# Gates of a product-key expert layer: scattered into a DRAM table instead of built by one-hot matmuls

## The chip, the cores and the metric

The kernel runs on one core of a Trainium2 chip. The metric is the device time of one execution in microseconds. The five engines run side by side, each through its own queue of instructions in a fixed order: TensorE (PE; PEld are its weight loads), VectorE (DVE), ScalarE (ACT), GpSimd (POOL) and SyncE (SP, which here only issues DMAs). They wait for each other through semaphores.

## The reference, cut to what matters

Two transformer blocks over 272 and then 256 tokens of width 1024, all in float32. The change sits in the last part of the first block, a layer that routes each token to a few of 16384 experts:

```python
q = (xt @ w_q).reshape(BLOCK, PEER_HEADS, PEER_QDIM)            # 8 heads, 2 x 128 wide
s1 = einsum('chd,nd->chn', q[..., :half], keys1)                # 128 scores per head
s2 = einsum('chd,nd->chn', q[..., half:], keys2)                # 128 scores per head
t1, i1 = top_k(s1, 16);  t2, i2 = top_k(s2, 16)
cand = t1[..., :, None] + t2[..., None, :]                      # 256 sums
cidx = i1[..., :, None] * 128 + i2[..., None, :]                # expert number
ts, sel = top_k(cand, 16)
idx = take_along_axis(cidx, sel);  g = softmax(ts)
act = gelu(einsum('chkd,cd->chk', u[idx], xt))
return einsum('chk,chkd->cd', g * act, v[idx])
```

So a token has 8 heads of 16 experts each: 128 gates in all, of which two heads may name the same expert; then their gates add up.

## The kernel before, in words

**Dense form.** The kernel does not gather rows of `u` and `v`. It computes `u @ x` for all 16384 experts and 256 tokens (the first product), multiplies by a dense table of gates that is zero nearly everywhere, and multiplies the result with all of `v` (the second product). The table lives in the SBUF tile `C` of 128 x 128 x 256: partition `j` is the second key index, the middle index `a` the first key index, the last index the token. In the first product 64 steps `n` (two values of `a` each) fill it.

**Streams.** Every weight tile of 1 MB goes through `st.units` (line 115): SP loads it into one of two `raw` buffers (line 125), ACT copies a half of it in a rounded format into one of three `ws` buffers (line 138), DVE subtracts to get the rest (line 141), and PE runs three matmuls per pair (`mm3`, lines 157 to 159). One step `n` of the first product takes two such halves, 48 matmuls of 128x256.

**Routing** (lines 726 to 785). After each head's scores (line 848) DVE has two top-16 searches per head and token half (lines 732 to 737), the sums of the candidates (745), a third search (751 to 755), and a look-up of the expert numbers by comparison, product and sum over 16x50 elements (760 to 764). It runs for a whole token half `t` (128 tokens, 8 heads) at a time. PE then transposes key indices and gates (783), so that they lie in `idT` with one column per token.

**Scatter** (lines 787 to 806). For four tokens at a time DVE compares (789) to make one-hot rows of the second key index, ACT (795, 796) or DVE (798) makes one-hot rows of the first key index scaled by the gate, and PE multiplies the two (801): 128x128 gates of one token per matmul, 256 matmuls in all. DVE multiplies the part of `C` that is already there by it (804), ACT copies the rest into `C` (806), to be multiplied when the first product gets there (874).

**Order.** `work()` is a generator that yields after each piece with an estimated cost. After each step `n`, `advance` (line 831) takes pieces from it until their costs reach a limit that grows by `BUD` = 3.2 per step. `G` (line 723) ties a piece behind the last split of the weight stream. So the pieces of routing and scatter lie between the weight splits, in each engine's fixed queue.

Of the kernel before, what the change touches and what calls it, by code (L numbers as in the profile page):

```python
# [21 lines left out]
T = 256  # L22
# [11 lines left out]
NACT = 2  # L34
BUD = 3.2
RC = 1.3
R1STEP = 2
# [29 lines left out]
def _body(nc, tc, ctx, a, out, dbg):  # L67
# [30 lines left out]
    xd = dp.tile([128, 2, D], F32, name="xd")  # L98
    nc.sync.dma_start(X[0], a["x"][0:128])
# [4 lines left out]
    class Stream:  # L104
        def __init__(self):
            self.pools = [(gp, 2, 3)]
            self.gate = None
            self.reset()
# [6 lines left out]
        def units(self, src, alloc=None, eng=None, behind=None):  # L115
# [9 lines left out]
            nc.sync.dma_start(dst, src)  # L125
            res = []
# [140 lines left out]
    # ------------------------------------------------------------------ block 1  # L267
    with ExitStack() as s1:
# [14 lines left out]

        g1 = gain(G_NORM1, bp, bufs=1)
# [43 lines left out]
        # recurrent branch input and causal conv  # L328
# [15 lines left out]
        # latent projections  # L344
# [58 lines left out]
        # log_sigmoid(lambda) * 8  # L403
# [18 lines left out]
        # recurrent gates  # L422
# [41 lines left out]
        # keys, values, queries  # L464
# [90 lines left out]
        # recurrent output  # L555
# [7 lines left out]
        # attention, with other products between the heads  # L563
# [126 lines left out]
        finish(1)  # L690
        dump("h1", X[0])
        stop("h1")

    # ------------------------------------------------------------------ PEER
    with ExitStack() as s2:
# [8 lines left out]
        idT = cp.tile([128, 3, T], F32, name="idT")  # L704
        niota = cp.tile([128, 128], F32, name="niota")
        nc.vector.tensor_scalar(niota, iota, -1.0, None, ALU.mult)
        Tv = C[:, 112:120, 192:224].rearrange("p h (s k) -> p h s k", s=2)
        If = C[:, 120:128, 192:224].rearrange("p h (s k) -> p h s k", s=2)
        Iu = C[:, 120:128, 192:224].bitcast(U32).rearrange("p h (s k) -> p h s k", s=2)
        cand = C[:, 96:104, 128:128 + NCAND]  # L710
        cidx = C[:, 104:112, 128:128 + NCAND]
        eq = C[:, 112:128, 128:128 + NCAND]
        tsv = C[:, 112:120, 224:240]
        posu = C[:, 120:128, 224:240].bitcast(U32)
        posf = C[:, 120:128, 240:256]
        wks = [cp.tile([128, 128], F32, name=f"wk{i}") for i in range(2)]
        sl = cp.tile([128, 3, 8, 16], F32, name="sl")
        sli = cp.tile([128, 2, 128], I32, name="sli")

        def bc(v, k):  # L720
            return v.unsqueeze(3).to_broadcast([128, v.shape[1], v.shape[2], k])
# [4 lines left out]
        def routing(t):  # L726
            V = nc.vector
            for s in range(16):
                h, k = s // 2, s % 2
                src = sc[t][:, s, :]  # L730
                wk1 = wks[s % 2]
                G(V.max(Tv[:, h, k, 0:8], src))
                V.max_index(Iu[:, h, k, 0:8], Tv[:, h, k, 0:8], src)
                V.match_replace(wk1, Tv[:, h, k, 0:8], src, -3.4e38)
                yield 0.5
                G(V.max(Tv[:, h, k, 8:16], wk1))
                V.max_index(Iu[:, h, k, 8:16], Tv[:, h, k, 8:16], wk1)
                yield 0.35
            V.tensor_copy(If, Iu)
            V.tensor_scalar(If[:, :, 0, :], If[:, :, 0, :], 128.0, None, ALU.mult)  # L740
            yield 0.6
            for src, dst in ((Tv, cand), (If, cidx)):
                for i0, ni, nj, o in CAND:
                    d = dst[:, :, o:o + ni * nj].rearrange("p h (i j) -> p h i j", i=ni)
                    V.tensor_tensor(out=d, in0=bc(src[:, :, 0, i0:i0 + ni], nj),
                                    in1=src[:, :, 1, 0:nj].unsqueeze(2).to_broadcast([128, 8, ni, nj]), op=ALU.add)
                yield 1.6
            for h in range(8):
                c = cand[:, h, :]
                wk1 = wks[h % 2]  # L750
                G(V.max(tsv[:, h, 0:8], c))
                V.max_index(posu[:, h, 0:8], tsv[:, h, 0:8], c)
                V.match_replace(wk1[:, :NCAND], tsv[:, h, 0:8], c, -3.4e38)
                V.max(tsv[:, h, 8:16], wk1[:, :NCAND])
                V.max_index(posu[:, h, 8:16], tsv[:, h, 8:16], wk1[:, :NCAND])
                yield 0.8
            V.tensor_copy(posf, posu)
            fidx = sl[:, 0]
            for h in range(8):
                G(V.tensor_tensor(out=eq, in0=posf[:, h, :].unsqueeze(2).to_broadcast([128, 16, NCAND]),  # L760
                                  in1=iota[:, :NCAND].unsqueeze(1).to_broadcast([128, 16, NCAND]), op=ALU.is_equal))
                yield 0.9
                G(V.tensor_tensor(out=eq, in0=eq, in1=cidx[:, h, :].unsqueeze(1).to_broadcast([128, 16, NCAND]), op=ALU.mult))
                V.tensor_reduce(fidx[:, h, :], eq, AX.X, ALU.add)
                yield 1.8
            f2 = fidx.rearrange("p h k -> p (h k)")
            V.tensor_copy(sli[:, 0], f2)
            V.tensor_scalar(sli[:, 1], sli[:, 0], 127, None, ALU.bitwise_and)
            V.tensor_scalar(sli[:, 0], sli[:, 0], 7, None, ALU.logical_shift_right)
            V.tensor_scalar(sl[:, 0].rearrange("p h k -> p (h k)"), sli[:, 0], -1.0, None, ALU.mult)  # L770
            V.tensor_copy(sl[:, 1].rearrange("p h k -> p (h k)"), sli[:, 1])
            yield 0.8
            e = sl[:, 2]
            V.tensor_tensor(out=e, in0=tsv, in1=tsv[:, :, 0:1].to_broadcast([128, 8, 16]), op=ALU.subtract)
            nc.scalar.activation(e, e, AF.Exp)
            sm = small.tile([128, 8], F32, name="sm", tag="sm", bufs=2)
            V.tensor_reduce(sm, e, AX.X, ALU.add)
            V.reciprocal(sm, sm)
            V.tensor_tensor(out=e, in0=e, in1=sm.unsqueeze(2).to_broadcast([128, 8, 16]), op=ALU.mult)
            yield 0.6  # L780
            p = ps("pt")
            for j in range(3):
                nc.tensor.transpose(p[:, j * 128:(j + 1) * 128], sl[:, j].rearrange("p h k -> p (h k)"), ident)
            nc.scalar.activation(idT[:, :, t * 128:(t + 1) * 128], p[:, :384].rearrange("p (j t) -> p j t", j=3), AF.Copy)
            yield 0.1

        def scatter(t0, bound):
            oh = x_tile().rearrange("p (q w) -> p q w", q=4)
            G(nc.vector.tensor_tensor(out=oh[:, :, 0:128], in0=iota.unsqueeze(1).to_broadcast([128, 4, 128]),
                                      in1=idT[:, 1, t0:t0 + 4].unsqueeze(2).to_broadcast([128, 4, 128]), op=ALU.is_equal))  # L790
            for k in range(4):
                t = t0 + k
                o = oh[:, k, 128:256]
                if k < NACT:
                    nc.scalar.activation(o, iota, AF.Abs, bias=idT[:, 0, t:t + 1])
                    nc.scalar.activation(o, o, AF.Relu, bias=idT[:, 2, t:t + 1], scale=-4.0)
                else:
                    G(nc.vector.tensor_scalar(o, niota, idT[:, 0, t:t + 1], idT[:, 2, t:t + 1], ALU.is_equal, ALU.mult))
            p = ps("pm")
            for k in range(4):  # L800
                nc.tensor.matmul(p[:, k * 128:(k + 1) * 128], oh[:, k, 0:128], oh[:, k, 128:256], start=True, stop=True)  # L801
            v = p.rearrange("p (q a) -> p a q", q=4)
            cs = C[:, 0:bound, t0:t0 + 4]
            nc.vector.tensor_tensor(out=cs, in0=v[:, 0:bound, :], in1=cs, op=ALU.mult)
            if bound < 128:
                nc.scalar.activation(C[:, bound:128, t0:t0 + 4], v[:, bound:128, :], AF.Copy)

        r0, r1 = routing(0), routing(1)

        class Scattered:  # L810
            done = 0

        def work():
            for c in r0:
                yield c * RC
            for k in range(64):
                if k == 32:
                    for c in r1:
                        yield c * RC
                scatter(4 * k, work.bound)  # L820
                Scattered.done = 4 * k + 4
                yield 1.1 + work.bound / 240
                for _ in range(R1STEP if k < 32 else 0):
                    c = next(r1, None)
                    if c:
                        yield c * RC

# [3 lines left out]
        def advance(limit):  # L831
            while spent[0] < limit:
                c = next(todo, None)
                if c is None:
                    return
# [652 lines left out]
```

## Time and profile before

| what | value |
|---|---|
| three timed runs | 2146.55, 2145.16, 2147.39 us; median 2146.55 |
| span of the profiled execution | 2144.5 us; the runs lie 0.7 to 2.9 us above it |
| mean granted TensorE clock | 0.995 |
| busy share of POOL | 5% |
| HBM traffic | 360.29 MB read, 2.10 MB written, 169 GB/s over the span |

A busy share is an average over the whole span. The first block takes the first 290 us, the projection `wpq` and the scores end near 346 us, the first product runs to 771 us, the second product to about 1123 us, and the second block takes the rest. What a change is worth is read from the stage it touches.

### The profile page before, as it was taken

Reading aid. Unit: us, or ns where it says so; the run is one execution under the profiler, and the core shown is the slowest. Engines: PE = TensorE matmul, PEld = TensorE weight load, DVE = VectorE, ACT = ScalarE, POOL = GpSimd, SP = SyncE. Lnnn points to the kernel's source line nnn. Section 1 sums busy time; section 2 is a strip of 40 time slices with the busy share of each in tenths; the row PEclk is TensorE's granted clock in tenths of the full one; section 3 lists DMA queues with packets and bytes.
Section 4 is the critical chain, followed back from the end, with each engine's and each line's share of the span. In section 5 each row is a group of like instructions: output and inputs, shape, how many; then the busy total and the mean of one; then the engine's idle time right before and its main releaser. Section 6 shows DMA issues by size and latency. Waiting matters only on the chain.

```text
span 2144.5 us, 31162 instructions
## 1 busy us (share of the span) xinstructions
PE 2093.2 (98%) x12401; PEld 1838.8 (86%) x12401; DVE 1395.0 (65%) x2361; ACT 1143.7 (53%) x1903; POOL 113.6 (5%) x112
## 2 busy tenths in 40 slices
PE   8989999999999999999999999999999999999998
PEld 7889989999999988888887887887887888887886
DVE  6685668888888865555557555967556554756554
ACT  5875444576657744444446444665445444555443
POOL 2010000000000000000000000840000000000000
PEclk9999999999999999999999999999999999999999
DMA  6432554544443445555576554316554654634551
GB/s 212 160 124 96 175 175 163 185 154 159 171 162 137 147 167 191 183 195 184 189 261 230 190 184 170 118 40 248 193 180 170 217 179 157 225 120 165 188 183 72
DMA packets 65361, 365.57 MB, mean 170 GB/s; under 512 B 6704, under 2 KB 8880, under 8 KB 33472
## 3 DMA queue, kind: packets, MB, share of 16 engines
q1 hardware_dynamic: 65216, 363.59, 49.1%
q8 instruction: 97, 1.59, 0.3%
q14 instruction: 48, 0.39, 0.1%
HBM read 360.29 MB, written 2.10 MB: 169 GB/s over the span
## 4 chain that ended last, share of the span: by engine, by line
PE 87%; DVE 5%; ACT 4%; DMA 2%; issue 1%; POOL 1%; SPq 0%; POOLq 0%; DVEq 0%; ACTq 0%
PE pa L157 18%; PE pa L159 18%; PE pa L158 18%; PE pm L157 8%; PE pm L159 8%; PE pm L158 8%; PE pm L801 3%; DVE ws L141 2%; PE pt L194 2%; PE pm L1106 1%; ACT ws L138 1%; DMA raw<-in_ffn_dram 1%; POOL rr L180 1%; ACT sq L170 1%; PE pm L590 1%
## 5 line engine op out<-in xcount | busy, mean ns | idle before, releaser
L141 DVE TENSOR_TENSOR ws<-raw,ws 128x1024 fp32r<-128x1024 f32 (+1 forms) x653 | 795.7, 1225 | 519.8 <-ACT ws L138 514.9
L138 ACT ACTIVATE ws<-raw 128x1024 fp32r<-128x1024 f32 (+1 forms) x657 | 689.3, 1057 | 548.2 <-PE pa L159 347.2
L157 PE MATMUL pa<-xT,ws 128*128 128x256 f32 x1280 | 365.0, 286 | 0.0
L159 PE MATMUL pa<-xT,ws 128*128 128x256 f32 x1280 | 360.9, 282 | 0.0
L158 PE MATMUL pa<-xT,ws 128*128 128x256 f32 x1280 | 360.8, 282 | 0.0
L157 PE MATMUL pm<-ws,xT 128*128 128x512 f32 (+1 forms) x768 | 298.9, 389 | 2.3 <-ACT xT L162 2.3
L159 PE MATMUL pm<-ws,xT 128*128 128x512 f32 (+1 forms) x768 | 294.7, 384 | 2.3 <-DVE xT L163 2.2
L158 PE MATMUL pm<-ws,xT 128*128 128x512 f32 (+1 forms) x768 | 293.8, 383 | 1.1 <-DVE ws L141 1.0
L157 PEld LDWEIGHTS pa<-xT,ws 128*128 128x128 f32 x1280 | 242.1, 189 | 0.3 <-ACT xT L162 0.3
L158 PEld LDWEIGHTS pa<-xT,ws 128*128 128x128 f32 x1280 | 242.0, 189 | 0.0
L159 PEld LDWEIGHTS pa<-xT,ws 128*128 128x128 f32 x1280 | 241.9, 189 | 0.0
L157 PE MATMUL pa<-ws,ch 128*128 128x512 f32 x512 | 201.3, 395 | 1.0 <-ACT ch L162 1.0
L158 PE MATMUL pa<-ws,ch 128*128 128x512 f32 x512 | 201.9, 395 | 0.0
L159 PE MATMUL pa<-ws,ch 128*128 128x512 f32 x512 | 201.5, 394 | 0.0
L159 PEld LDWEIGHTS pm<-ws,xT 128*128 128x128 f32 x768 | 144.8, 189 | 33.0 <-DVE xT L163 3.5
L157 PEld LDWEIGHTS pm<-ws,xT 128*128 128x128 f32 x768 | 144.9, 189 | 30.3 <-ACT xT L162 4.0
L158 PEld LDWEIGHTS pm<-ws,xT 128*128 128x128 f32 x768 | 144.8, 189 | 29.9 <-DVE ws L141 2.5
L157 PE MATMUL pa<-ws,hT 128*128 128x512 f32 x352 | 141.9, 403 | 0.6 <-ACT hT L162 0.5
L159 PE MATMUL pa<-ws,hT 128*128 128x512 f32 x352 | 137.9, 394 | 0.2
L158 PE MATMUL pa<-ws,hT 128*128 128x512 f32 x352 | 137.7, 391 | 0.0
L180 POOL TENSOR_TENSOR rr<-rs,mhalf 128x1 f32<-128x1 f32 (+1 forms) x36 | 28.7, 798 | 1938.9 <-DVE rs L178 1938.9
L157 PEld LDWEIGHTS pa<-ws,ch 128*128 128x128 f32 x512 | 96.4, 188 | 23.6 <-ACT ch L162 1.2
(390 smaller groups left out, 3202.1 us busy)
## 6 DMA issues: line engine op xcount, KB each, us to landing
raw<-in_ffn_dram SPq DMA_DIRECT2D x132, 1024.0 KB, 4.9
raw<-in_peer_u_dram SPq DMA_DIRECT2D x64, 1024.0 KB, 4.9
raw<-in_peer_v_dram SPq DMA_DIRECT2D x64, 1024.0 KB, 4.9
raw<-in_win_dram SPq DMA_DIRECT2D x16, 1024.0 KB, 4.8
gain<-in_gains_dram SPq DMA_DIRECT2D x17, 512.0 KB, 5.6
raw<-in_wpq_dram SPq DMA_DIRECT2D x8, 1024.0 KB, 5.0
raw<-in_wcin_dram SPq DMA_DIRECT2D x8, 1024.0 KB, 4.9
raw<-in_wrnn_dram SPq DMA_DIRECT2D x4, 1024.0 KB, 4.9
```

The lines of the kernel that those rows point to most:

```text
L138: i = nc.scalar.activation(hi, r, AF.Copy)
L141: self.last = (eng or nc.vector).tensor_tensor(out=lo, in0=r, in1=hi.bitcast(F32), op=ALU.subtract)
L157: nc.tensor.matmul(o, wh, xh, start=first, stop=False)
L158: nc.tensor.matmul(o, wh, xl, start=False, stop=False)
L159: nc.tensor.matmul(o, wl, xh, start=False, stop=last)
L170: nc.scalar.activation(sq[:rows, :p.shape[-1]], p, AF.Square, accum_out=ss[:rows, i:i + 1])
L180: nc.gpsimd.tensor_tensor(out=r2[:rows], in0=r[:rows], in1=mhalf[:rows], op=ALU.pow)
L194: nc.tensor.transpose(p[:, j * rows:(j + 1) * rows], src[:rows, (b + j) * 128:(b + j + 1) * 128], ident[:rows, :rows])
L590: nc.tensor.matmul(sp[:, :nk], qT[h // 8][:, h % 8, t * 128:(t + 1) * 128], kT[h // 8][:, h % 8, :nk], start=True, stop=True)
L801: nc.tensor.matmul(p[:, k * 128:(k + 1) * 128], oh[:, k, 0:128], oh[:, k, 128:256], start=True, stop=True)
L1106: in_turn(nc.tensor.matmul(p[:, :T], dg, u[:, k:k + T], start=k == 0, stop=k == 30))
```

## The change

- A DRAM tile `gd` of 128 x (128 x 256) takes the place of the one-hot products. Sixteen DMAs of 1 MB each set it to zero during the first block. They come from the SP queue, one after each call of the weight stream from the 8th on.
- Routing is done for one head and one token half at a time, heads in the outer loop, as soon as the scores of a head are there. Its scratch tiles lie outside `C`.
- The expert number is computed as an address in `gd` that includes the token. The 16 gates of a head and token half are added into `gd` by 16 indirect DMAs of 128 elements each, issued by POOL: 256 in all. Those of one group are declared independent, those of the next head of the same tokens wait for the ones before. In POOL's queue each indirect DMA also waits for the completion of the one eight places ahead of it.
- The transposes, the one-hot rows, the one-hot matmuls and both ways of multiplying in the first product go. `C` holds the activated first product alone.
- In the second product POOL reads 512 KB of `gd` for four values of `a` at a time (32 reads), and DVE multiplies that part of `C` by it, one group ahead of its use.
- The softmax uses one ACT instruction per head and token half, with the sum accumulated there.
- `BUD` goes from 3.2 to 3.0 without the factor 1.3 on routing; before the first product a limit of 1.5 per head holds.

Core of the diff (line numbers of the new kernel differ by a few to some tens from those of the old one):

```diff
+    gd = dp.tile([128, 128 * T], F32, name="gd")
...
+            self.calls += 1
+            if self.aside is not None:
+                self.aside(self.calls)
...
+        zero = tmp("zero", [128, 512], 1)
+        nc.gpsimd.memset(zero, 0.0)
+        def clear(i):
+            i -= ZFROM
+            if 0 <= i < ZN:
+                w = 128 * T // ZN
+                nc.sync.dma_start(gd[:, i * w:(i + 1) * w].rearrange("p (r w) -> p r w", w=512),
+                                  zero.unsqueeze(1).to_broadcast([128, w // 512, 512]))
...
+            V.tensor_scalar(If[:, z, 0, :], Iu[:, z, 0, :], float(T), tokf[:, t:t + 1], ALU.mult, ALU.add)
+            V.tensor_scalar(If[:, z, 1, :], Iu[:, z, 1, :], 128.0 * T, None, ALU.mult)
+            for src, dst in ((Tv, cand), (If, cidx)):
+                for i0, ni, nj, o in CAND:
+                    d = dst[:, z, o:o + ni * nj].rearrange("p (i j) -> p i j", i=ni)
+                    V.tensor_tensor(out=d, ...)
...
+            nc.scalar.activation(e, tsv[:, z, :], AF.Exp, bias=nm, accum_out=sm)
...
+            for k in range(16):
+                i = nc.gpsimd.indirect_dma_start(gflat, bass.IndirectOffsetOnAxis(ap=slot[:, t, h, k:k + 1], axis=0),
+                                                 gate[:, t, h, k:k + 1], None, compute_op=ALU.add)
...
-        def scatter(t0, bound):
-            oh = x_tile().rearrange("p (q w) -> p q w", q=4)
-            G(nc.vector.tensor_tensor(out=oh[:, :, 0:128], ..., op=ALU.is_equal))
-            for k in range(4):
...
-            for k in range(4):
-                nc.tensor.matmul(p[:, k * 128:(k + 1) * 128], oh[:, k, 0:128], oh[:, k, 128:256], start=True, stop=True)
...
+        def work():
+            for h in range(8):
+                yield h, 0.0
+                for t in range(2):
+                    for c in routing(t, h):
+                        yield h, c
...
-            advance(13.6 + BUD * (n + 1) if n < 62 else 1e9)
+            nc.scalar.activation(C[:, 2 * n:2 * n + 2, :], p.rearrange("p (a t) -> p a t", a=2), AF.Gelu_apprx_tanh)
+            advance(WQBUD * 7 + BUD * (n + 1) if n < 36 else 1e9)
...
+        def gates_of(g):
+            v = x_tile().rearrange("p (a t) -> p a t", a=4)
+            nc.gpsimd.dma_start(v, gd[:, 4 * T * g:4 * T * (g + 1)].rearrange("p (a t) -> p a t", a=4))
+            return v
+        def gated_c(g):
+            c = C[:, 4 * g:4 * g + 4, :]
+            nc.vector.tensor_tensor(out=c, in0=c, in1=gl.pop(0), op=ALU.mult)
+            if g + 2 < 32:
+                gl.append(gates_of(g + 2))
```

How the change moves instructions is read from the order of each engine's queue. The first place is DVE in the middle of the first product. `ws<-raw,ws` are the splits of the weight stream, the others belong to the scatter; before, with the kernel's old line numbers:

```order
L141 TENSOR_TENSOR ws<-raw,ws 128x1024 x2
L874 TENSOR_TENSOR C<-hb,C 128x2x196
L804 TENSOR_TENSOR C<-pm,C 128x112x4
L789 TENSOR_TENSOR x<-iota,idT 128x4x128
L804 TENSOR_TENSOR C<-pm,C 128x112x4
L798 TENSOR_SCALAR x<-niota,idT 128x128 x2
```

And now, near step 23 of the first product, the later part of one head's routing (`tsv` the 16 best sums, `eqs` the look-up, `gate` the gates), with the new line numbers:

```order
L148 TENSOR_TENSOR ws<-raw,ws 128x1024
L771 MAX tsv<-cand 128x8
L772 MAX_INDEX posu<-tsv,cand 128x8
L773 MATCH_REPLACE wk_3145<-tsv,cand 128x50
L777 TENSOR_SCALAR nm<-tsv 128x1
L774 MAX tsv<-wk_3145 128x8
L780 MAX_INDEX posu<-tsv,wk_3145 128x8
L781 CAST posf<-posu 128x16
L783 TENSOR_TENSOR eqs<-posf,iota 128x800
L786 TENSOR_TENSOR eqs<-eqs,cidx 128x800
L790 RECIPROCAL sm<-sm 128x1
L148 TENSOR_TENSOR ws<-raw,ws 128x1024 x2
```

Routing now fills the room between the splits in steps 0 to 34 in place of the scatter's pieces, and none is left after the split of step 34. The first address (`slot`) is finished on DVE between the splits of the sixth and the seventh of the eight `wpq` tiles.

The second place is POOL's queue around this layer. Before, ten of the small powers of the norms (line 180) follow each other there, two ahead of this layer and eight behind it; then comes the convolution of the second block (1147):

```order
L363 TENSOR_TENSOR qr_979<-ropet 128x16x16
L180 TENSOR_TENSOR rr<-rs,mhalf 128x1 x10
L1147 TENSOR_TENSOR pw<-ud,pv 128x1024
L1150 TENSOR_TENSOR pw<-pw 128x512 x2
L1147 TENSOR_TENSOR pw<-ud,pv 128x1024
```

Now:

```order
L381 TENSOR_TENSOR qr_986<-ropet 128x16x16
L187 TENSOR_TENSOR rr<-rs,mhalf 128x1 x2
L740 IOTA tok 128x2
L794 DMA gd<-gate,slot 4194304x1 x256
L864 DMA x<-gd 128x1024 x32
L187 TENSOR_TENSOR rr<-rs,mhalf 128x1 x8
L1132 TENSOR_TENSOR pw<-ud,pv 128x1024
```

The 256 indirect DMAs and the 32 reads stand between the second and the third of these powers, all in one queue, the reads behind the last indirect DMA.

The third place is SP's queue early in the first block, where weight tiles (`raw`) are loaded. Before:

```order
L125 DMA raw<-in_win_dram 128x2048 x2
L565 DMA mask<-in_mask_dram 128x416
L90 DMA iota<-in_iota_dram 128x128
L186 DMA gain<-in_gains_dram 128x1024
L125 DMA raw<-in_win_dram 128x2048 x2
L125 DMA raw<-in_wkn_dram 128x2048
```

Now:

```order
L129 DMA raw<-in_win_dram 128x2048 x2
L298 DMA gd<-zero 128x4x512
L129 DMA raw<-in_win_dram 128x2048
L298 DMA gd<-zero 128x4x512 x3
L129 DMA raw<-in_win_dram 128x2048
L298 DMA gd<-zero 128x4x512
L129 DMA raw<-in_wkn_dram 128x2048
```

Five of the sixteen clearing DMAs come here, three of them in a row ahead of one weight tile; three small loads have moved behind.

## Rows read from the trace of the kernel before

**Rows 1.** The page, part 1: busy us (share of the span) and instructions of each engine.
```profile
PE 2093.2 (98%) x12401; PEld 1838.8 (86%) x12401; DVE 1395.0 (65%) x2361; ACT 1143.7 (53%) x1903; POOL 113.6 (5%) x112
```
**Rows 2.** The chain that ended last, first line by engine, second by line.
```profile
PE 87%; DVE 5%; ACT 4%; DMA 2%; issue 1%; POOL 1%; SPq 0%; POOLq 0%; DVEq 0%; ACTq 0%
PE pa L157 18%; PE pa L159 18%; PE pa L158 18%; PE pm L157 8%; PE pm L159 8%; PE pm L158 8%; PE pm L801 3%; DVE ws L141 2%; PE pt L194 2%; PE pm L1106 1%; ACT ws L138 1%; DMA raw<-in_ffn_dram 1%; POOL rr L180 1%; ACT sq L170 1%; PE pm L590 1%
```
**Rows 3.** Busy us by stretch; the columns are in the first line.
```profile
core 0: us, PE busy (x) PEld busy (x) DVE busy (x) ACT busy (x) POOL busy (x), PEclk, DMA share, GB/s
305.00:352.00 47.00, 47.00 (x403) 47.00 (x402) 38.26 (x139) 20.33 (x30) 0.00 (x0) 1.00 0.47 158
352.00:433.00 81.00, 81.00 (x686) 81.00 (x684) 70.71 (x170) 40.40 (x49) 0.00 (x0) 1.00 0.55 184
439.00:770.00 331.00, 330.62 (x2815) 330.21 (x2813) 275.62 (x622) 218.91 (x505) 0.00 (x0) 1.00 0.45 153
771.50:1107.00 335.50, 335.50 (x1445) 272.05 (x1444) 182.30 (x153) 156.70 (x152) 0.00 (x0) 1.00 0.55 188
```
**Rows 4.** ACT in order of time, ends of steps: start us, us, engine, line [idle before].
```profile
351.63 0.60 ACT L876 ACTIVATE C<-pa 128x512 f32<-128x512 f32 x1 [0.49 <-PE pa L159]
358.22 0.60 ACT L876 ACTIVATE C<-pa 128x512 f32<-128x512 f32 x1 [1.73 <-PE pa L159]
426.57 0.60 ACT L876 ACTIVATE C<-pa 128x512 f32<-128x512 f32 x1 [1.78 <-PE pa L159]
432.27 0.60 ACT L876 ACTIVATE C<-pa 128x512 f32<-128x512 f32 x1 [1.79 <-PE pa L159]
770.55 0.58 ACT L873 ACTIVATE hb<-pa 128x512 f32<-128x512 f32 x1
```
**Rows 5.** The chain of waits late in the first product: start us, us, what.
```profile
755.60 1.78 PE pm L801 x16
763.08 0.89 PE pm L801 x8
```
**Rows 6.** DVE groups by form: count, busy us, mean ns, idle before them.
```profile
L141 DVE TENSOR_TENSOR ws<-raw,ws 128x1024 fp32r<-128x1024 f32 x46 | 56.0, 1220 | 24.2 <-ACT ws L138 24.2
L840 DVE COPY C<-pa 128x256 f32<-128x256 f32 x16 | 6.0, 414 | 0.2
```
**Rows 7.** DVE in order of time near 350 us.
```profile
349.77 1.22 DVE L141 TENSOR_TENSOR ws<-raw,ws 128x1024 fp32r<-128x1024 f32 x1
350.91 0.29 DVE L736 MAX8 C<-wk 128x8 f32<-128x128 f32 x1
356.08 0.53 DVE L745 TENSOR_TENSOR C<-C 128x32 f32<-128x32 f32 x4
```
**Rows 8.** POOL in order of time, then DVE beside the last two.
```profile
1123.33 0.55 POOL L180 TENSOR_TENSOR rr<-rs,mhalf 128x1 f32<-128x1 f32 x1 [833.29 <-DVE rs L178]
1132.38 1.46 POOL L180 TENSOR_TENSOR rr<-rs,mhalf 128x1 f32<-128x1 f32 x1 [5.12 <-DVE rs L178]
1453.88 2.60 POOL L180 TENSOR_TENSOR rr<-rs,mhalf 128x1 f32<-128x1 f32 x1 [10.80 <-DVE rs L178]
1132.21 1.22 DVE L141 TENSOR_TENSOR ws<-raw,ws 128x1024 fp32r<-128x1024 f32 x1
1454.85 1.22 DVE L141 TENSOR_TENSOR ws<-raw,ws 128x1024 fp32r<-128x1024 f32 x1
```
**Rows 9.** DMA issues: count, KB each, median us from issue to landing.
```profile
raw<-in_win_dram SPq DMA_DIRECT2D x16, 1024.0 KB, 4.8
gain<-in_gains_dram SPq DMA_DIRECT2D x17, 512.0 KB, 5.6
```
**Rows 10.** Table loads of ACT in the first product.
```profile
L876 ACT ACT_TABLE_LOAD  x2: 1283/1283/1283, 349.9 to 379.4; - x2
```
**Rows 11.** Waits of PE up to 295 us: total us, times, longest.
```profile
PE pa L159 <- DVE ws L141: 5.6, 3, 2.7
```

More of the change, by code (lines that the diff above doesn't have):

```diff
@@ L33 @@
 NCAND = 50
[L34 to L37, printed above, removed]
+BUD = 3.0
+WQBUD = 1.5
+ZFROM = 8
+ZN = 16
 NTAP = (16, 16, 16, 16)
@@ L107, in __init__ @@
             self.gate = None
+            self.calls = 0
+            self.aside = None
             self.reset()
@@ L690, in _body @@
         finish(1)
+        st.aside = None
+        assert st.calls >= ZFROM + ZN
         dump("h1", X[0])
@@ L711, in _body @@
[L711 to L721, printed above, removed]
+        NC = 2
@@ new lines, in _body @@
+        wks = [cp.tile([128, 128], F32, name=f"wk{i}") for i in range(NC)]
+        Tv = cp.tile([128, NC, 2, 16], F32, name="Tv")
+        Iu = cp.tile([128, NC, 2, 16], U32, name="Iu")
+        If = cp.tile([128, NC, 2, 16], F32, name="If")
+        cand = cp.tile([128, NC, NCAND], F32, name="cand")
+        cidx = cp.tile([128, NC, NCAND], F32, name="cidx")
+        tsv = cp.tile([128, NC, 16], F32, name="tsv")
+        posu = cp.tile([128, NC, 16], U32, name="posu")
+        posf = cp.tile([128, NC, 16], F32, name="posf")
@@ new lines, in _body @@
+        fid = cp.tile([128, NC, 16], F32, name="fid")
+        eqs = cp.tile([128, 16, NCAND], F32, name="eqs")
+        gate = cp.tile([128, 2, 8, 16], F32, name="gate")
+        slot = cp.tile([128, 2, 8, 16], I32, name="slot")
+        tok = cp.tile([128, 2], I32, name="tok")
+        tokf = cp.tile([128, 2], F32, name="tokf")
+        nc.gpsimd.iota(tok, [[128, 2]], base=0, channel_multiplier=1)
+        nc.vector.tensor_copy(tokf, tok)
+        gflat = gd.rearrange("p (e o) -> (p e) o", o=1)
@@ L723, in G, with routing @@
         def G(i):
             after(i, st.last)
-        def routing(t):
+        def routing(t, h):
             V = nc.vector
[L728 to L741, printed above, removed]
+            z = t
+            for k in range(2):
+                src = sc[t][:, 2 * h + k, :]
+                wk1 = wks[z]
+                G(V.max(Tv[:, z, k, 0:8], src))
+                V.max_index(Iu[:, z, k, 0:8], Tv[:, z, k, 0:8], src)
+                V.match_replace(wk1, Tv[:, z, k, 0:8], src, -3.4e38)
+                yield 0.6
+                G(V.max(Tv[:, z, k, 8:16], wk1))
+                V.max_index(Iu[:, z, k, 8:16], Tv[:, z, k, 8:16], wk1)
+                yield 0.4
+            V.tensor_scalar(If[:, z, 0, :], Iu[:, z, 0, :], float(T), tokf[:, t:t + 1], ALU.mult, ALU.add)
+            V.tensor_scalar(If[:, z, 1, :], Iu[:, z, 1, :], 128.0 * T, None, ALU.mult)
@@ L757, in routing @@
[L757 to L765, printed above, removed]
@@ L775, in routing @@
[L775 to L783, printed above, removed]
@@ L808, in _body @@
[L808 to L826, printed above, removed]
+                    d = dst[:, z, o:o + ni * nj].rearrange("p (i j) -> p i j", i=ni)
@@ new lines, in routing @@
+            nm = small.tile([128, 1], F32, name="nm", tag="nm", bufs=2)
+            sm = small.tile([128, 1], F32, name="sm", tag="sm", bufs=2)
+            V.tensor_scalar(nm, tsv[:, z, 0:1], -1.0, None, ALU.mult)
+            e = gate[:, t, h, :]
+            nc.scalar.activation(e, tsv[:, z, :], AF.Exp, bias=nm, accum_out=sm)
+            V.max_index(posu[:, z, 8:16], tsv[:, z, 8:16], wk1[:, :NCAND])
+            V.tensor_copy(posf[:, z, :], posu[:, z, :])
+            yield 0.9
+            G(V.tensor_tensor(out=eqs, in0=posf[:, z, :].unsqueeze(2).to_broadcast([128, 16, NCAND]),
+                              in1=iota[:, :NCAND].unsqueeze(1).to_broadcast([128, 16, NCAND]), op=ALU.is_equal))
@@ new lines, in routing @@
+            yield 0.9
+            G(V.tensor_tensor(out=eqs, in0=eqs, in1=cidx[:, z, :].unsqueeze(1).to_broadcast([128, 16, NCAND]), op=ALU.mult))
+            yield 0.9
+            G(V.tensor_reduce(fid[:, z, :], eqs, AX.X, ALU.add))
+            V.tensor_copy(slot[:, t, h, :], fid[:, z, :])
+            V.reciprocal(sm, sm)
+            V.tensor_scalar(e, e, sm, None, ALU.mult)
+            yield 1.2
+            for k in range(16):
+                i = nc.gpsimd.indirect_dma_start(gflat, bass.IndirectOffsetOnAxis(ap=slot[:, t, h, k:k + 1], axis=0), gate[:, t, h, k:k + 1], None,
+                                                 compute_op=ALU.add)
+                for key in [(t, h)] + [(1 - t, g) for g in range(h + 1)]:
+                    tc.declare_no_dep(i.ins, group="gates%d.%d" % key, reason="other elements")
+                tc.add_to_no_dep_group("gates%d.%d" % (t, h), i.ins)
@@ L828, in _body, with advance @@
+        def work():
+            for h in range(8):
+                yield h, 0.0
+                for t in range(2):
+                    for c in routing(t, h):
+                        yield h, c
         todo = work()
         spent = [0.0]
[L831 to L835, printed above, removed]
-                spent[0] += c
+        nxt = [next(todo)]
+        def advance(limit, heads=8):
+            while nxt[0] is not None and nxt[0][0] < heads and spent[0] < limit:
+                spent[0] += nxt[0][1]
+                nxt[0] = next(todo, None)
@@ L867, in _body @@
                 scores(7)
[L868 to L880 removed]
+            nc.scalar.activation(C[:, 2 * n:2 * n + 2, :], p.rearrange("p (a t) -> p a t", a=2), AF.Gelu_apprx_tanh)
+            advance(WQBUD * 7 + BUD * (n + 1) if n < 36 else 1e9)
+        assert nxt[0] is None
         acc = [[ps("pa") for _ in range(2)] for _ in range(2)]
```

73 lines of the change are left out of this document (15 added, 58 removed).

## The prediction

> **What bounds the kernel now.** I read four views in this order: the page's busy times, the chain of waits, the busy time by stretch, and the pace of the steps. The page has PE at 2093.2 us of a span of 2144.5 [rows 1], and the chain that ended last is PE for 87% [rows 2]. That is an average, so the stage of the change counts. In the stretch from 439 to 770 us, where the scatter runs, PE is busy 330.62 of 331.00 us, DVE 275.62, POOL not at all, at full clock [rows 3]. The same holds before the scatter starts (352 to 433 us: PE 81.00 of 81.00, DVE 70.71) and in the second product (335.50 of 335.50). So each matmul that goes in this stage gives its time back, as long as nothing else becomes late.
>
> **What the change removes.** The pace without scatter is read from the ends of the steps: step 1 at 358.22, step 14 at 432.27 us, which is 74.05 us for 13 steps, 5.70 us each [rows 4]. Step 0 ended at 351.63, and the last one, step 63, at 770.55. At the bare pace the 63 steps between would take 358.9 us; the last scores (8 matmul records, 6.59 us for step 1 instead of 5.70) add 0.9. The stage took 418.9. The rest, 59.2 us, is what scatter and transposes cost PE. A second way agrees: the chain has 8 records of the one-hot product as a piece of 0.89 us and 16 as 1.78 [rows 5]; 64 such pieces are 57.0 us, and the six transposes and small waits make up the other two. I take 59.2 us off.
>
> **What it adds on DVE.** The pieces of routing stay, and the scatter's DVE work goes, but routing now has to fit into the room beside the splits within 35 steps. The room: two splits start 1.14 us apart from what follows them (349.77 and 350.91 [rows 7]), so a step leaves 5.70 - 2.28 = 3.42 us. The need: from 305 to 433 us DVE was busy 38.26 + 70.71 = 109.0 us [rows 3]; 45 splits (128 us at half a step of 2.85) at 1.22 us make 54.9, and the 16 copies of the projection 6.0 [rows 6]. What is left, 48 us, is the routing of one token half, 96 for both. By head, the 14 sums of candidates are issued 16 x 14 times instead of 2 x 14: 196 more at 0.13 us (four in 0.53 us [rows 7]) are 26 us. Seven small instructions per head and half in place of some eleven per half are about 90 more, 12 us. Together 134 us, an estimate, of which a tenth (58 of 624 instructions in the order) falls into the projection before. So 121 us in 35 steps, 3.46 us against 3.42 of room: DVE is full and about 1.4 us short, and bunches add something. From below the cost is nothing, since `ws` buffers give some lead; from above, with instructions that wait for the one before them a quarter dearer (1.22 us for a split that costs 1.14 in a stream, 0.29 for a search that costs 0.20), routing is 168 us, 151 of it in the stage, and 151 + 35 x 2.28 = 231 against 199 us of steps: 32 us late. I take 3 us, near the measured pace of routing.
>
> **ACT.** The sixteen exponentials now stand between activations of the other kind. One table load is 1.28 us [rows 10]; some 28 of them are 36 us in 35 steps, 1.0 us a step. With two copies of 1.06 and one activation of 0.60 [rows 4] a step needs 3.8 of 5.70 us. Nothing, while ACT has this room; if an exponential has to wait for DVE at a bad moment, the copy behind it and then PE wait, which is part of the 32 us above.
>
> **The clearing DMAs.** Sixteen of 1 MB stand in SP's queue among the weight loads of the first block. One such transfer lands in 4.8 us [rows 9], and at one place three stand ahead of a weight tile. In all of the first 295 us PE waited for splits in its main products 5.6 us, in three waits [rows 11], so loads have some lead, though not everywhere. Bounds: nothing, and 3 x 4.8 = 14.4 us. I take 2.
>
> **The second product.** DVE gets 32 products of the size of a split, 39 us over the stage of some 350; it is busy 182.30 of 335.50 us there, so it goes to about 65%. POOL's 32 reads of 512 KB add a quarter to the 2 MB of weights per group, and the DMA engines are at 0.55 [rows 3]. Both are one group (about 21 us) ahead of their use and cost nothing; without that lead each group would pay 1.2 us, 39 in all.
>
> **The indirect DMAs: the open price.** None is in the trace. The first address is ready when DVE is through the seventh `wpq` tile at the latest, near 330 us by the place in the order, and the first product would now end at 770.6 - 59.2 + 3 + 2 = 716 us. The first read of the table needs all 256 of them and then lands in about 5.6 us (512 KB [rows 9]). So they are hidden if one takes POOL up to (716 - 330 - 5.6) / 256 = 1.49 us. The last address comes with step 34, near 548 us, so the pace of routing does not bind. The nearest rows are POOL's smallest instruction, over 128x1: 0.55 us with DVE idle beside it, 1.46 beside one split, 2.60 beside two instructions of DVE, ending 0.41 us after DVE's in both cases [rows 8]. DVE is busy five sixths of this stretch while routing runs, and less than half of it afterwards. The bounds are 0.55 and 2.60; I take 1.46, the row with one split beside it, which matches two splits per step. Then POOL is through at 330 + 374 = 704 us and the table is there at 710, 6 us before it is needed. The cover is thin: each 0.1 us more per DMA is 26 us later.
>
> The rows show POOL held until DVE's instruction ends. [...]
>
> **Sum.** Against the profiled execution's span of 2144.5: - 59.2 + 3 + 2 = 2090.3 us. The median of the runs lies 2.05 us above that span, so 2092 us.
>
> **Rivals.**
> - *POOL is late, and the kernel is slower.* Mechanism: each indirect DMA waits for DVE, the first read of `gd` stands behind all of them in POOL's queue, DVE's first product with the gates waits for the read, and PE's second product for DVE. For it: 1.46 and 2.60 us in rows 8, and DVE at 85% there. Against it: from step 35 on DVE runs only two splits a step, 2.4 of 5.7 us, and 163 us of the stage are left. At the middle of the two rows, 2.03 us, the table is there at 330 + 520 + 5.6 = 856 us, 140 late: 2232 us. At 2.60 it is 1001, 2377 us. It decides from 1.70 us on: then the 54 us of net gain are gone.
>
> [...]
>
> - *DVE is the bound of the first product.* For it: 85 to 87% busy before, and need equal to room above. Against it: PE did not wait with DVE at 87%. Price: the 32 us bound instead of 3, 2121 us.
> - *The matmuls were hidden anyway,* and the time stays at 2146: then PE would have had idle time in the stage, but it has 0.4 of 331 us. PE would have to wait elsewhere for what it no longer does.
>
> **How the numbers follow.** The forecast (2080 to 2115) has 0.58. DVE as the bound 0.11. POOL late 0.28: of that 0.05 between 1.49 and 1.70 us and still faster, 0.02 about equal, 0.21 slower. Hidden anyway 0.03, 0.01 of it equal and 0.02 slower. Within 0.2% (4.3 us) is about what a measurement of this kernel cannot tell from no change. So faster 0.74, same 0.03, slower 0.23. The range: down to 2080, where nothing that is added costs and the scheduling of the first block gains some us; up to 2180, which takes in DVE's bound and POOL up to 1.83 us per DMA. The likeliest case alone is 2080 to 2115.
>
> **What would show it.** Right: no matmul between the three of the weight stream, steps of 5.7 us from 1 to 63, the first product ending near 716 us, POOL's last indirect DMA before that, and PE going on into the second product with no more than a us or two of waiting. Steps of 6 us or more up to step 34 with DVE ahead of PE in the waits: DVE was mis-sized. A gap of PE between the products, released through the read of `gd`: the price of the indirect DMAs was wrong, and its size divided by 256 says by how much. PE waits on splits before 250 us that were not there: the clearing DMAs.

## The result, and the profile after

The changed kernel takes 2385.31 us (median of 4 runs, 2384.30 to 2388.88) against 2145.86 us before: a ratio of 1.1115, interval 1.1102 to 1.1128. The forecast of 2092 us and its range up to 2180 us missed it; the rival "POOL is late" had the way from POOL to PE, but at its middle price a wait of 140 us, half of what came. The matmuls did go. The page of the changed kernel, part 1, answers to [rows 1]:

```profile
PE 2040.5 (86%) x11883; PEld 1784.1 (75%) x11883; DVE 1345.4 (56%) x2372; ACT 1088.2 (46%) x1588; POOL 562.7 (24%) x402
```

PE has 52.7 us less to do, and is busy for 86% of the span instead of 98%. The busy time by stretch shows where it stands idle (columns as in [rows 3]: PE, PEld, DVE, ACT, POOL, then PE's granted clock, DMA share, GB/s):

```profile
352.00:433.00 81.00, 81.00 (x683) 80.81 (x682) 79.82 (x314) 54.16 (x69) 69.96 (x37) 1.00 0.67 179
439.00:567.00 128.00, 127.80 (x1074) 127.33 (x1073) 114.97 (x421) 81.61 (x99) 110.01 (x60) 1.00 0.71 188
567.00:847.00 280.00, 0.50 (x5) 0.29 (x3) 3.22 (x3) 1.54 (x2) 228.42 (x151) 0.51 0.25 4
847.00:1006.00 159.00, 152.59 (x1246) 150.71 (x1246) 97.95 (x83) 67.84 (x77) 15.12 (x29) 0.98 0.78 271
```

Up to 567 us PE is as full as before, although DVE is busy 79.82 of 81 us instead of 70.71. Then everything but POOL stops for 280 us. It stops in the middle of the first product, and not behind it. ACT in order of time, ends of steps 0, 1, 37, 38 and 63, answers to [rows 4]:

```profile
354.49 0.60 ACT L847 ACTIVATE C<-pa 128x512 f32<-128x512 f32 x1 [0.42 <-issue]
361.07 0.60 ACT L847 ACTIVATE C<-pa 128x512 f32<-128x512 f32 x1 [1.78 <-PE pa L166]
...
567.29 0.60 ACT L847 ACTIVATE C<-pa 128x512 f32<-128x512 f32 x1 [1.78 <-PE pa L166]
855.19 0.60 ACT L847 ACTIVATE C<-pa 128x512 f32<-128x512 f32 x1 [1.81 <-PE pa L166]
...
1006.17 0.58 ACT L847 ACTIVATE C<-pa 128x512 f32<-128x512 f32 x1
```

Who holds PE is read backwards through two engines. PE waits for a split of DVE (waits of PE from 346 to 1010 us: total us, times, longest):

```profile
PE pa L166 <- DVE ws L148: 285.4, 10, 279.9
```

DVE in order of time (three splits, then the stop) shows that the next split stood behind a product of `C` with the gates, and that the product waited for the read of the table:

```profile
554.15 1.23 DVE L148 TENSOR_TENSOR ws<-raw,ws 128x1024 fp32r<-128x1024 f32 x1 [1.14 <-ACT ws L145]
557.48 1.22 DVE L148 TENSOR_TENSOR ws<-raw,ws 128x1024 fp32r<-128x1024 f32 x1 [2.11 <-ACT ws L145]
559.85 1.23 DVE L148 TENSOR_TENSOR ws<-raw,ws 128x1024 fp32r<-128x1024 f32 x1 [1.14 <-ACT ws L145]
843.78 2.45 DVE L869 TENSOR_TENSOR C<-C,x 128x1024 f32<-128x1024 f32 x2 [282.70 <-DMA x<-gd]
846.15 2.35 DVE L148 TENSOR_TENSOR ws<-raw,ws 128x1024 fp32r<-128x1024 f32 x2
```

POOL in order of time shows what the read waited for: the indirect DMAs, one after the other, until 837.8 us (the first, three from the time when routing is over on DVE, the last, and the first two reads; `...` marks rows left out):

```profile
329.63 2.53 POOL L794 DMA_INDIRECT gd<-gate,slot  x1 [34.19 <-DVE slot L789]
...
554.84 1.95 POOL L794 DMA_INDIRECT gd<-gate,slot  x1 [0.30 <-issue]
557.10 1.54 POOL L794 DMA_INDIRECT gd<-gate,slot  x1 [0.31 <-issue]
...
560.79 1.70 POOL L794 DMA_INDIRECT gd<-gate,slot  x1 [0.31 <-issue]
...
836.23 1.54 POOL L794 DMA_INDIRECT gd<-gate,slot  x1 [0.31 <-issue]
839.84 1.17 POOL L864 DMA_DIRECT2D x<-gd  x2 [2.07 <-issue]
```

POOL's indirect DMAs as groups (count, busy us, mean ns, idle before them), first up to 566 us (DVE busy 216.8 of 236 us from 330 us on), and then up to 838 us, where DVE stands idle:

```profile
L794 POOL DMA_INDIRECT gd<-gate,slot x109 | 203.6, 1868 | 67.1 <-DVE slot L789 34.2 <-issue 31.4 <-DVE cidx L766 0.3
L794 POOL DMA_INDIRECT gd<-gate,slot x148 | 228.3, 1543 | 45.1 <-issue 45.1
```

The products stood there already in the order of the instructions. DVE's queue in the changed kernel, from the end of routing on:

```
L791 TENSOR_SCALAR gate<-gate,sm 128x16
L788 TENSOR_REDUCE fid<-eqs 128x16
L789 CAST slot<-fid 128x16
L148 TENSOR_TENSOR ws<-raw,ws 128x1024 x6
L869 TENSOR_TENSOR C<-C,x 128x1024 x2
L148 TENSOR_TENSOR ws<-raw,ws 128x1024 x2
L869 TENSOR_TENSOR C<-C,x 128x1024 x2
```

Six splits (three steps) behind the last address come the first two products, and then two more between the splits of every step, 24 in all by step 49. In the program text they stand behind the first product. But the rows of `C` for small `a` are complete after a few steps, nothing ties these products to the splits, and the scheduler moved them forward; why to this place is not shown. In the end all 32 reads were issued and 31 of the 32 products done before the last step of the first product ended, though the change was meant to have them in the second.

The sum by stretches: step 0 ends 2.9 us later than before (354.49 against 351.63). Steps 1 to 37 take 206.22 us for 36, or 5.73 each, 1.0 us more than at 5.70. The gap is 279.9 us. From step 37 to 63 at 5.70 us and 0.8 for the end would be 149.0 us; it took 438.9, so 10.0 more than the gap. Of those, 5.5 are nine further waits of PE and about 2 come from some 20 matmuls at half pace after the gap (one every 0.21 us instead of 0.12); the other 2.5 lie in steps 39 to 49, and their cause is not shown. So - 59.2 + 2.9 + 1.0 + 279.9 + 10.0 = 234.6; the last step ended 235.6 us later (1006.17 against 770.55), and the span grew by 238.0.

### The profile page after: what moved, and what is told of

Same layout as the page of the kernel before. It is cut to its first block, busy times and chain, and to the rows that moved or that the text cites. A ratio compares the mean times of both kernels' runs of the same rounds, so it can differ in the third digit from the quotient of the medians.

```text
span 2382.5 us, 30211 instructions
## 1 busy us (share of the span) xinstructions
PE 2040.5 (86%) x11883; PEld 1784.1 (75%) x11883; DVE 1345.4 (56%) x2372; ACT 1088.2 (46%) x1588; POOL 562.7 (24%) x402
## 4 chain that ended last, share of the span: by engine, by line
PE 53%; DVE 6%; DMA 3%; issue 1%; ACT 1%; POOL 1%; POOLq 0%; DVEq 0%; ACTq 0%; SPq 0%
PE pa L166 10%; PE pa L164 10%; PE pa L165 10%; PE pm L164 7%; PE pm L166 7%; PE pm L165 7%; DMA x<-gd 2%; DVE pa L1116 2%; DVE ws L148 2%; PE pt L201 1%; POOL rr L187 1%; ACT sq L177 0%; DMA raw<-in_ffn_dram 0%; POOL gd L794 0%; DVE xn L220 0%
## 5 line engine op out<-in xcount | busy, mean ns | idle before, releaser
L794 POOL DMA_INDIRECT gd<-gate,slot x256 | 430.4, 1681 | 112.0 <-issue 76.3
L869 DVE TENSOR_TENSOR C<-C,x 128x1024 f32<-128x1024 f32 x32 | 39.2, 1225 | 310.1 <-DMA x<-gd 303.0
L164 PE MATMUL pa<-ws,hT 128*128 128x512 f32 x352 | 141.2, 401 | 0.6 <-ACT hT L169 0.5
L165 PE MATMUL pa<-ws,hT 128*128 128x512 f32 x352 | 137.6, 391 | 0.0
```

The source lines that it names most:

```text
L164: nc.tensor.matmul(o, wh, xh, start=first, stop=False)
L165: nc.tensor.matmul(o, wh, xl, start=False, stop=False)
L794: i = nc.gpsimd.indirect_dma_start(gflat, bass.IndirectOffsetOnAxis(ap=slot[:, t, h, k:k + 1], axis=0), gate[:, t, h, k:k + 1], None, comp ...
L869: nc.vector.tensor_tensor(out=c, in0=c, in1=gl.pop(0), op=ALU.mult)
```

## The experiments

The theory after the traces had two parts. (1) POOL needs 508.2 us for 256 indirect DMAs, 1.985 us each, where the forecast took 1.46. (2) The products in DVE's queue make the table due at the splits of step 38, near 567 us, and not at the end of the first product. Three runs undo the parts singly and together, two ask what the price is made of, one tries the clears alone, and two look for a kernel that beats both.

**Products tied behind the splits.**

```diff
-            nc.vector.tensor_tensor(out=c, in0=c, in1=gl.pop(0), op=ALU.mult)
+            after(nc.vector.tensor_tensor(out=c, in0=c, in1=gl.pop(0), op=ALU.mult), st.last)
```

> The changed kernel, with each product of C with the gates tied behind the last weight split that stands ahead of it in the program, so that none stands in DVE's queue inside the first product. Theory (two parts: POOL needs 508 us for 256 indirect DMAs whatever comes behind, and in the changed kernel DVE's products stood in its queue from the splits of step 38 on): the first product ends near 715 us, the table is there at about 844, PE waits some 130 us between the two products, and the time is 2385 - 280 - 12 + 132 = about 2227 us. Rival (PE stopped at 567 us for want of weights, because the indirect DMAs crowd out the weight loads): the order of the products changes nothing, PE still stops near 567, 2385 us. Second rival (DVE in the way of POOL: with DVE now busy with splits from 567 to 715 the indirect DMAs of that stretch cost 2.17 instead of 1.85 us each): the table is some 26 us later, 2253 us.

Measured 2227.67 us, ratio 1.0376 (1.0358 to 1.0393). All 58 splits behind the last address (two in each of 29 steps) now come ahead of the first product with the gates, and PE runs through to the end of the first product. Its waits from 346 to 1100 us have one large entry, now between the two products:

```profile
PE pa L164 <- ACT ch L169: 134.7, 1, 134.7
```

So the order alone cost 2385.31 - 2227.67 = 157.6 us. The weights were not crowded out. The second rival fell too: POOL's groups by form (count, busy us, mean ns), up to 566 us, from there to 714 us, and from 715 us on, show that splits alone (DVE busy 63.7 of 148 us) raise the mean little, from 1.542 us with DVE idle to 1.593 us:

```profile
L794 POOL DMA_INDIRECT gd<-gate,slot x108 | 202.2, 1872 | 66.9 <-DVE slot L789 34.2 <-issue 30.8 <-DMA gd<-gate,slot 0.6
L794 POOL DMA_INDIRECT gd<-gate,slot x79 | 125.8, 1593 | 24.1 <-issue 23.2 <-DMA gd<-gate,slot 0.6 <-DVE ws L148 0.3
L794 POOL DMA_INDIRECT gd<-gate,slot x71 | 109.5, 1542 | 21.7 <-issue 21.4 <-DMA gd<-gate,slot 0.3
```

**Half of the indirect DMAs, products where the change has them.**

```diff
-            for k in range(16):
+            for k in range(8):
                 i = nc.gpsimd.indirect_dma_start(...)
```

> The changed kernel with 8 of the 16 indirect DMAs per head and token half left out (the 8 smaller gates are not added), the products where they were. Theory: POOL is through by about 605 us instead of 838, DVE and PE stop at 567 as before but only until about 611; the gap is 44 us, and the time 2385 - 236 = about 2149 us. If the wait were set by routing (last address at 548) the gap would be under 5 us and the time near 2105; if by something that does not scale with the number of DMAs, it stays above 2300.

Measured 2159.16 us, in one run. The last indirect DMA starts at 605.8 us (summary of line 794: least, median and longest ns of the 128, first and last start), and PE's longest wait for a split is 53.3 us instead of 279.9:

```profile
L794 POOL DMA_INDIRECT gd<-gate,slot x128: 1535/1555/3524, 329.6 to 605.8; - x128
PE pa L166 <- DVE ws L148: 61.6, 9, 53.3
```

The gap is 9 us more than expected: PE stopped at 562.5 us, not 567, and went on at 615.9, not 611. The mechanism holds: with the table there some 100 us before PE could be through with the first product (716 us), the kernel is still slower than before.

**Both edits.** The two diffs above together.

> Both edits: half of the indirect DMAs left out and the products tied behind the splits. Theory: the table is there near 611 us, the first product ends near 715, PE goes on without a gap, and the rest of the sum (59.2 off, 3 for clears, 1 for DVE) holds: 2090 to 2096 us. Rival (the matmuls were hidden anyway, or clears, routing by head and reads cost more than the two products showed): 2110 us or more.

Measured 2094.32 us, ratio 0.9755 (0.9739 to 0.9772). PE's longest wait from 346 to 1100 us is 1.0 us, and the steps are at 5.70 us from step 36 on. The wait between the two products is now:

```profile
PE pa L164 <- ACT ch L169: 1.0, 1, 1.0
```

This is the forecast's own figure (2092), reached where both of its failed steps are mended; half of the gates are missing from it. Step 0 ends at 355.83 us, the last at 717.82. ACT's first work behind the second product (`diag`) comes 338.4 us after the last step, here and in the kernel before:

```profile
717.82 0.58 ACT L847 ACTIVATE C<-pa 128x512 f32<-128x512 f32 x1
1056.26 2.44 ACT L1090 ACTIVATE diag<-ident,pv 128x128 f32<-128x128 f32 x8
```
```profile
1108.94 2.43 ACT L1105 ACTIVATE diag<-ident,pv 128x128 f32<-128x128 f32 x8
```

So the 32 reads and 32 products cost nothing in the second product, as forecast. From the last step to the end of the program it takes 1376.1 us against 1374.0 before; these 2 us lie in the second block, and the kernel with the clears alone, which reads nothing, has them too (1376.7).

**64 partitions per indirect DMA.** The products are tied.

```diff
-...(ap=slot[:, t, h, k:k + 1], axis=0), gate[:, t, h, k:k + 1], ...
+...(ap=slot[0:64, t, h, k:k + 1], axis=0), gate[0:64, t, h, k:k + 1], ...
```

> The products tied behind the splits, and each of the 256 indirect DMAs carries 64 partitions instead of 128 (the gates of half of the tokens are not added). If the 1.84 us from one indirect DMA to the next (DVE idle) are a fixed price per DMA, POOL still ends near 838 us and the time is that of the tied kernel, about 2227 us. If they go by the element, 0.9 to 1.1 us each, POOL is through with the last address, near 570 us, and the time is 2090 to 2096 us. Something between would split the price into a fixed part and one per element.

Measured 2208.18 us in one run: nearly the fixed price. The summary of this line (least, median and longest ns of the 256):

```profile
L794 POOL DMA_INDIRECT gd<-gate,slot x256: 1392/1397/3175, 329.5 to 816.4; - x128
```

Half of the elements save 0.145 of 1.54 us. That is 2.3 ns per element; carried on to no element at all, 1.25 us of POOL plus the 0.30 between two of them would be left, an estimate.

**Plain writes.** The products are tied, and `compute_op=ALU.add` is left out of the call.

> The kernel with the tied products, each indirect DMA a plain write instead of an addition (gates that fall on the same expert are not added up). If the price of 1.54 + 0.30 us is POOL's own work per DMA, nothing changes: 2227 us, mean on POOL 1.54 us with DVE idle. If reading the old value back is part of it, or of what holds the queue, POOL is through earlier by at least 0.1 us per DMA, 26 us, and the time is at most 2201 us.

Measured 2105.17 us in one run. The theory expected no change here, while the expectation's other branch, at most 2201 us, came true:

```profile
L794 POOL DMA_INDIRECT gd<-gate,slot x256: 954/959/2882, 329.8 to 709.2; - x128
```

With no DVE instruction in the way, an addition costs POOL 1.54 us and a plain write 0.96. The two also differ in the packets of POOL's DMA queue, for the additions, for 64 partitions and for plain writes:

```profile
q0 software_dynamic: 41472, 16.93, 6.4%
```
```profile
q0 software_dynamic: 25088, 16.86, 4.4%
```
```profile
q0 software_dynamic: 12800, 16.93, 2.4%
```

The run with half of the DMAs has 23040, so the 128 left out were 18432 packets, 144 each, and the 32 reads are 4608. That leaves 80 per DMA with 64 partitions and 32 per plain write. The price falls with the packets, but not in proportion: from 144 to 80 it falls by 0.145 us, from 80 to 32 by 0.44. So what an addition is dearer by is measured, and its cause is not shown. PE's pace in this run was 5.76 us a step instead of 5.70, for which no cause is shown; over 63 steps that is some 4 us.

**The clears alone, in the kernel before.**

```diff
+            self.calls += 1
+            if self.aside is not None:
+                self.aside(self.calls)
...
+        st.aside = clear
```

> The kernel before, with nothing but the table and its sixteen clearing DMAs of 1 MB added at the same places of SP's queue in the first block; nothing reads the table. Theory: the 2.9 us by which step 0 of the first product ended later come from them: 2145.7 + 2.9 = 2148.6 us. Rival (they come from routing by head, which begins before step 0): within 0.5 us of 2145.7.

Measured 2150.57 us, ratio 1.0020 (1.0011 to 1.0029): 4.2 us. Step 0 ends at 353.76 us instead of 351.63, so 2.1 of them come ahead of it:

```profile
353.76 0.60 ACT L894 ACTIVATE C<-pa 128x512 f32<-128x512 f32 x1 [0.48 <-PE pa L165]
772.71 0.58 ACT L891 ACTIVATE hb<-pa 128x512 f32<-128x512 f32 x1
1111.10 2.44 ACT L1123 ACTIVATE diag<-ident,pv 128x128 f32<-128x128 f32 x8
```

Through both products nothing is added (the last step and `diag` are 2.2 us later as well); the rest comes in the second block, where no clearing DMA stands, and its cause is open. The clears are worth 2 to 4 us, and the rival falls.

**Half by DMA, half by matmul.** Tokens 128 to 255 go through a half-sized table, tokens 0 to 127 through the one-hot matmuls of the kernel before.

```diff
+            for h in range(8):
+                for c in routing(1, h):       # tokens 128 to 255: 128 indirect DMAs
+                    yield h, c
+            for h in range(8):
+                for c in routing(0, h):       # tokens 0 to 127
+                    yield 7, c
+            turn()                            # transposes of ids and gates
...
+            for k in range(32):
+                scatter(4 * k, work.bound)
...
```

> The whole computation, done half and half: tokens 128 to 255 by 128 indirect DMAs into a table half as large (8 clearing DMAs, 32 reads of 256 KB, products tied behind the splits), tokens 0 to 127 by one-hot matmuls as in the kernel before. Theory: the 128 DMAs are through by about 620 us, before the first product ends, as with half of them left out; PE saves half of what the scatter cost it, 29.6 us, and the clears cost about half of 2.9 us: 2145.7 - 29.6 + 1.5 + 1 = about 2119 us, faster than both. Rival (DVE is full: routing by head, 121 us, 32 scatter groups and 128 splits in the first product): steps longer than 5.7 us while both lie there, 2130 us or more.

Measured 2122.53 us, ratio 0.9887 (0.9872 to 0.9902): faster than both. The last indirect DMA starts at 624.6 us, the first product ends at 747, and PE's only wait behind it is 1.0 us:

```profile
L804 POOL DMA_INDIRECT gd<-gate,slot x128: 1536/1565/3775, 330.5 to 624.6; - x128
PE pa L164 <- ACT ch L169: 1.0, 1, 1.0
```

It is 3.5 us above the expected 2119.

**Plain writes of sums.** All 256 as plain writes; the sum over earlier heads that name the same expert is made on DVE before the write. Routing may now run up to step 54, and the second token half goes first.

```diff
+                G(V.tensor_tensor(out=m, in0=fid[:, t, h, :]..., in1=fid[:, t, 0:h, :]..., op=ALU.is_equal))
+                G(V.tensor_tensor(out=m, in0=m, in1=gate[:, t, 0:h, :]..., op=ALU.mult))
+                G(V.tensor_reduce(out, m, AX.X, ALU.add))
+                V.tensor_tensor(out=out, in0=out, in1=e, op=ALU.add)
...
-                                                 compute_op=ALU.add)
```

> The whole computation with 256 plain indirect writes (0.96 us on POOL instead of 1.54): where an earlier head of the same token names the same expert, DVE finds it by comparing expert numbers and writes the sum of the gates, so the last write holds all. Products tied behind the splits. Theory: POOL is through near 711 us as in the run with plain writes, the first product ends near 717, PE waits a few us for the table at most, and DVE's extra comparisons, about 50 us, still fit beside the splits up to step 52: 2096 to 2106 us, faster than the mixed kernel's 2122. Rival (the comparisons make DVE the bound of the first product: 121 + 50 us of routing and 156 of splits in 359): steps of 6 us or more while routing runs, last address after 670 us, 2115 us or more.

Measured 2116.66 us, ratio 0.9865 (0.9849 to 0.9882), the fastest of the whole computations here. DVE is busy 283.27 of 291 us while routing runs, and PE still does not wait there:

```profile
352.00:643.00 291.00, 290.97 (x2449) 290.60 (x2449) 283.27 (x834) 175.48 (x212) 236.45 (x180) 1.00 0.55 182
```

It misses its expected 2096 to 2106 by a wait for the table, since the last write starts at 729.4 us, 20 us later than in the run with plain writes alone. PE's wait between the products:

```profile
PE pa L164 <- ACT ch L169: 22.9, 1, 22.9
```

While routing runs, a write takes POOL 1.31 us on average (236.45 us for 180) instead of 0.96.

## Why the prediction was wrong, step by step

| step of the prediction | forecast | measured |
|---|---|---|
| matmuls and transposes go | - 59.2 us | steps at 5.70 to 5.73 us without them; the kernel with both mends, which lacks half of the gates, is 51 us faster than before |
| routing by head on DVE | + 3 | + 1.0 over steps 1 to 37, with DVE at 98% |
| table loads of ACT | 0 | 0: no wait of PE on ACT in the first product |
| clearing DMAs | + 2 | + 2.9 at step 0; 4.2 alone |
| reads and products in the second product | 0 | 0 once they lie there: 338.4 us from the last step to `diag`, as before |
| price of an indirect DMA, from one to the next | 1.46 us | 1.985 us |
| when the table is due | 716 us | 567 us |

**The step that failed first is the deadline.** "... the first product would now end at 770.6 - 59.2 + 3 + 2 = 716 us. ... So they are hidden if one takes POOL up to (716 - 330 - 5.6) / 256 = 1.49 us." The end was right: 717.82 with half of the DMAs and the products tied. But the table was due when DVE's queue came to the first product with the gates. The prediction placed the 32 products "one group (about 21 us) ahead of their use" in the second product, as the program's text has them, while in DVE's order two of them stand ahead of the splits of step 38. By its own price of 1.46 us, with the table at 710 us, PE would have stopped from 567 to about 713: an estimate of 2092 + 146 = 2238 us. So this step alone turns the sign, and the run with half of the DMAs shows it: POOL through at 607 us, and 2159 us. The break-even price against the old time was not 1.70 us, either. In the run with half of the DMAs POOL took 277.7 us, which is 1.08 us for each of 256, and the kernel was still 13.4 us slower than before: an estimate from that is 1.08 - 13.4 / 256 = 1.03 us.

**The second is the price.** 1.46 us was the row of a small arithmetic instruction beside one split [rows 8]. The indirect DMA takes 1.54 us on POOL with DVE idle (148 with a mean of 1.543 us between 566 and 838 us), and 0.30 us pass to the next: 1.84 us without any disturbance. The row had the wrong kind of instruction, and the 0.30 us between two DMAs was in no row. At 1.84 us POOL would have been through 471 us after 330, an estimate, instead of the forecast's 374. With the deadline mended, this step is worth 2227.67 - 2094.32 = 133.4 us, measured by leaving half of the DMAs out.

**The disturbance by DVE is real and small.** The rows above show it. The DMA at 554.84 starts beside a split that runs from 554.15 to 555.38, and ends 1.41 us after that split; the one at 560.79 ends 1.41 us after the split that ends at 561.08. They take 1.95 and 1.70 us instead of 1.54. Before 566 us the mean is 1.868 us, over 109 DMAs: (1.868 - 1.543) x 109 = 35 us of the 508. The other way round the rows show nothing added: the split at 557.48 starts 0.38 us into the DMA of 557.10 and takes 1.22 us, as it does alone. The disturbance is not what made POOL late.

Waiting for the completion of earlier DMAs did not make it late either. Of the 508.2 us POOL is busy for 430.4 and waits for the completion of an earlier indirect DMA for 0.3 in all. Nor is the price the same for every indirect DMA: with plain writes POOL gets through in 381 us.

**The rivals.** "POOL is late" had 0.28. Its chain from POOL through the read and DVE's product to PE was right; its first link, that each DMA waits for DVE, made up 35 of the 508 us, and its last, PE's second product, was the first product instead. Its formula at the measured price, 330 + 508 + 5.6 = 844 us and 2092 + 844 - 716 = 2220 us, comes near the tied kernel (2227.67), not the changed one, because it used the same deadline. Its 2377 us at 2.60 us per DMA lies near the measured time by chance, since POOL was through at 838 and not at 995 us. "DVE is the bound" fell: at 98% busy PE lost 1.0 us in 36 steps. "Hidden anyway" fell: 2094 us.

## What to carry to other kernels

Where a change adds a wait, find the waiting instruction in the order of its engine's queue, not in the program's text: the deadline is when that queue reaches it, and all that stands behind it there is late too, as the splits behind the first two products were here (DVE stood 282.70 us). An instruction whose data are early and whose last input is late has to be tied down explicitly, since a scheduler may move it forward, as it did here. An operation that no row shows has to be priced by its own kind, with the gap to the next one, times its count; and when its cover is thinner than the spread of its price, the range must reach as far as the dear end.

## What the runs showed of the hardware

An indirect DMA of 128 elements, one per partition, holds POOL for 1.54 us when it adds and 0.96 us when it writes, with no DVE instruction in the way, and the next one begins 0.30 us later; with 64 elements the addition takes 1.40 us. An addition of 128 elements makes 144 packets, a plain write 32. DVE at 97 to 99% of a stretch (283.27 of 291 us, 79.82 of 81) did not hold PE up, which was busy 290.97 and 81.00 us there. After the gap of 280 us (granted clock 0.51) PE came back with a matmul every 0.21 us, at a granted clock of 0.50 from 847.0 to 851.8 us. It was at one every 0.12 us from 851.9 us on, at 0.99 from 851.8 to 856.0, having worked without a break since 847.4:

```profile
847.42 0.58 PE L166 MATMUL pa<-xT,ws 128*128 128x256 f32 x1 [279.93 <-DVE ws L148]
847.80 0.42 PE L164 MATMUL pa<-xT,ws 128*128 128x256 f32 x1
848.02 0.41 PE L165 MATMUL pa<-xT,ws 128*128 128x256 f32 x1
...
851.86 0.30 PE L165 MATMUL pa<-xT,ws 128*128 128x256 f32 x1
851.99 0.28 PE L166 MATMUL pa<-xT,ws 128*128 128x256 f32 x1
852.11 0.28 PE L164 MATMUL pa<-xT,ws 128*128 128x256 f32 x1
```
